# Two-layer encoder on one core: seven block products for eight in twelve of the 44 pairs of W_up blocks

## The chip, the cores and the metric

The kernel runs on one core of a Trainium2 chip. The metric is the device time of the whole program in microseconds, the median of several runs. One further execution is recorded by the hardware profiler; its engines are PE (TensorE, matrix products), DVE (VectorE), ACT (ScalarE), POOL (GpSimd) and SP (SyncE, which issues most DMAs).

## The reference

Two layers, each an attention and Fourier block followed by a feed-forward block. The change touches the second of these alone:

```python
h = rmsnorm(x, norm2[l])                                   # 512 positions x 1024
up = dwconv_centred(h @ w_up[l], conv_w[l], conv_b[l])     # 1024 -> 5632, then 3 taps along positions
gate, val = up[..., :D_FF], up[..., D_FF:]                 # D_FF = 2816
x = x + (jax.nn.silu(gate) * val) @ w_down[l]
```

Everything is float32.

## The kernel before, in words

Activations lie with channels on the 128 partitions and the 512 positions in the free dimension. A float32 matrix is split into hi (rounded to the format in which PE multiplies fast) and lo = value - hi, and `mm3` makes each product from three matmuls: hi by hi, lo by hi, hi by lo (L120, L121, L122). ACT writes a hi, DVE the lo (`split` for activations, `wsplit` for weights: `whi` and `wlo`, five buffers each, half a tile of 1024 columns at a time). Raw weights arrive by DMA in `wraw`, three buffers.

The feed-forward block has 22 gate and 22 value tiles of W_up; gate tile `fi` and value tile `fi + 22` are a pair. For each tile a PSUM bank collects 8 x 3 matmuls of 128x512, so a pair has 48. A chunk, the 12 matmuls that use one `whi`/`wlo`, is half a tile. After a tile DVE multiplies by the positions' 1/rms (`rb2`, into a `tF` tile), ACT starts the convolution with its middle tap (`tF<-tF,pb`), and DVE adds the other two taps (L96, `scalar_tensor_tensor`). Once both tiles of a pair are there, ACT applies silu, the two are multiplied (by DVE in layer 0, by POOL in layer 1), and the result is split into `slab`, `pT` or `m4` for W_down. There are six `tF` buffers. The pairs come in two halves of eleven (`HALVES`); after each half follow the products with W_down, eight output tiles of 11 x 3 matmuls (the down stage). In layer 0's feed-forward block `presplit(1)` also prepares layer 1's projection weights, and layer 1's rope and other tables are loaded (`load_tables`).

The program is written as plain loops. When it is built, a scheduler fixes for each engine one order of instructions, and assigns buffers and waits; the engines then run independently, each in its own order.

Of the kernel before, what the change touches and what calls it, by code (L numbers as in the profile page):

```python
# [16 lines left out]
P = 128  # L17
# [15 lines left out]
RATE, STEP0 = 1, 12  # L33
FFN_BANKS = ("mm", "mm", "mm", "av", "sc", "sc")
HALVES = [(0, 11), (11, 11)]


def encoder_kernel(tc, t):
# [50 lines left out]
    def act(out, in_, func=AF.Copy, **kw):  # L89
        return nc.scalar.activation(out, in_, func, **kw)  # L90

    def tt(out, a, b, op, eng=None):
        return (eng or nc.vector).tensor_tensor(out, a, b, op=op)  # L93

    def stt(out, a, s, b, op0, op1):
        return nc.vector.scalar_tensor_tensor(out=out, in0=a, scalar=s, in1=b, op0=op0, op1=op1)  # L96
# [17 lines left out]
    def mm3(out, a, b, start, stop, after=None, **kw):  # L114

        with tc.issue_after(after) if after is not None else nullcontext():
            if len(a) == 1:
                nc.tensor.matmul(out, a[0], b[0], start=start, stop=stop, **kw)  # L118
                return
            nc.tensor.matmul(out, a[0], b[0], start=start, stop=False, **kw)  # L120
            nc.tensor.matmul(out, a[1], b[0], start=False, stop=False, **kw)  # L121
            nc.tensor.matmul(out, a[0], b[1], start=False, stop=stop, **kw)  # L122
# [20 lines left out]
    def wchunks(src, n, step=512, eng=None):  # L143
        raw = wload(src, n)
        return [wsplit(raw[:, c:min(c + step, n)], eng) for c in range(0, n, step)]

    kept = {}

    def presplit(l):

        late = []

        def keep(key, src):
            n = src.shape[-1]
            two = [temp(n, "tA", F32R) for _ in range(2)]
            split(two[0], two[1], src)
            kept[key] = [dp.tile([P, n], F32, tag=f"{key}{s}", name=nm("kept")) for s in range(2)]
            store()
            late.append(lambda: [nc.sync.dma_start(o, f(z)) for o, z in zip(kept[key], two)])

        def store():
            while late:
                late.pop()()

        def cols(src, n, step):
            def load():
                raw = temp(1024, "m4")
                nc.sync.dma_start(raw[:, :n], src)
                return [raw[:, c:c + step] for c in range(0, n, step)]
            return load  # L170

        def prepare(kind, raw):
            if kind == "u":
                return fold_wu(raw)
            return fold_wf(raw) if kind == "f" else raw

        jobs = []
        for grp in (1, 0):
            for kk in range(KT // 2):
                jobs.append((cols(t["w_qkv"][l, grp, kk], 768, 384), [f"qkv{grp}{2 * kk + i}" for i in range(2)]))  # L180
        for kk in range(KT // 2):
            jobs.append((lambda kk=kk: load_wu(l, kk, temp(1024, "m4")), [f"u{2 * kk + i}" for i in range(2)]))
        for j in range(NF):
            jobs.append((lambda j=j: [load_wf(l, j, temp(1024, "m4"))], [f"f{j}"]))
        for half in range(2):
            for mp in range(KT // 2):
                jobs.append((cols(t["w_o"][l, half, :, mp * 1024:(mp + 1) * 1024], 1024, 512),
                             [f"o{half}{2 * mp + i}" for i in range(2)]))
        got = jobs[0][0]()
        for n, (_, keys) in enumerate(jobs):  # L190
# [145 lines left out]
    def accum(tag="acc"):  # L336
        return cp.tile([P, 512], F32, tag=tag, name=nm(tag), bufs=1)
# [30 lines left out]
    def load_wu(l, kk, raw=None):  # L368

        raw = wtile() if raw is None else raw  # L370
        nc.sync.dma_start(raw.rearrange("p (k c) -> p k c", k=2),
                          t["w_in"][l, 2 * kk * P:2 * (kk + 1) * P, 0:FW].rearrange("(k p) c -> p k c", p=P))
        return [raw[:, k * 512:(k + 1) * 512] for k in range(2)]

    acc = accum()
    xg = [norm_tile(k, g1[:, 0, :], acc) for k in range(KT)]

    for l in range(L):
# [319 lines left out]
        rb2 = row_rstd(col_rstd(acc2, 1.0 / D))  # L698


        acc = accum()
        if l == 0:
            tabs, alts, wt = load_tables(1)
        ahead = presplit(l + 1) if l < L - 1 else iter(lambda: 0, 1)
        for f0, nf in HALVES:
            gu = []
            for fi in range(f0, f0 + nf):
                ys_ = []
                n = fi - f0
                for z in range(2):  # L710
                    m = fi + z * FT
                    w = wchunks(t["w_up"][l, m], 1024)
                    nps[0] += 1
                    o = psum(FFN_BANKS[nps[0] % len(FFN_BANKS)])
                    for k in range(KT):
                        mm3(o, [q[:, (k % 4) * P:(k % 4 + 1) * P] for q in w[k // 4]], [h2[k][:, s, :] for s in range(2)],
                            k == 0, k == KT - 1)
                    u = temp(512, "tF")
                    tt(u, o, rb2, ALU.mult)
                    y = temp(512, "tF")  # L720
                    act(y, u, AF.Identity, scale=cw[:, l, 1, m:m + 1], bias=cb[:, l, m:m + 1])
                    stt(y[:, 1:], u[:, :-1], cw[:, l, 0, m:m + 1], y[:, 1:], ALU.mult, ALU.add)
                    stt(y[:, :-1], u[:, 1:], cw[:, l, 2, m:m + 1], y[:, :-1], ALU.mult, ALU.add)
                    ys_.append(y)
# [36 lines left out]
            xg = nxt
# [88 lines left out]
```

## Time and profile before

| | us |
|---|---|
| median of 3 runs | 1057.18 (1056.22 to 1057.36) |
| profiled execution | 1056.14 |
| its span | 1054.3 |
| PE busy in the span | 1038.2 |
| DVE busy | 726.8 |
| ACT busy | 507.9 |
| up stages of layer 0, by the trace | 182 to 305 and 362 to 485 |
| up stages of layer 1 | 692 to 812 and 870 to 993 |

The time of an execution is its span and 1.84 us around it. In a group's row stand the line, engine and operation, then output and inputs by the program's names, the shape, the count; behind the first bar the busy time and the mean of one in ns, behind the second the engine's idle time before these instructions and what ended it. A timeline row begins with the start and the duration in us. Matmul durations overlap, so one reads the distance of their starts.

### The profile page before, as it was taken

Reading aid. Unit: us, or ns where it says so; the run is one execution under the profiler, and the core shown is the slowest. Engines: PE = TensorE matmul, PEld = TensorE weight load, DVE = VectorE, ACT = ScalarE, POOL = GpSimd, SP = SyncE. Lnnn points to the kernel's source line nnn. Section 1 sums busy time; section 2 is a strip of 40 time slices with the busy share of each in tenths; the row PEclk is TensorE's granted clock in tenths of the full one; section 3 lists DMA queues with packets and bytes.
Section 4 is the critical chain, followed back from the end, with each engine's and each line's share of the span. In section 5 each row is a group of like instructions: output and inputs, shape, how many; then the busy total and the mean of one; then the engine's idle time right before and its main releaser. Section 6 shows DMA issues by size and latency. Waiting matters only on the chain.

```text
span 1054.3 us, 14425 instructions
## 1 busy us (share of the span) xinstructions
PE 1038.2 (98%) x5107; PEld 873.2 (83%) x5107; DVE 726.8 (69%) x1384; ACT 507.9 (48%) x939; POOL 90.8 (9%) x164
## 2 busy tenths in 40 slices
PE   8998999999999999999999999999999999999998
PEld 8986778888888888888899887888888888888887
DVE  8878768697767777777519775478877336878632
ACT  5339755455444445455423785246554224454421
POOL 0004410000000000000000152001101000101100
PEclk9999999999999999999999999999999999999999
DMA  7232152332269833239856313333332333332241
GB/s 273 83 115 87 58 193 81 100 100 96 78 226 353 324 100 101 89 114 322 280 181 221 113 62 99 122 100 94 101 101 74 96 115 100 98 101 82 82 150 48
DMA packets 60475, 140.03 MB, mean 133 GB/s; under 512 B 6642, under 2 KB 22258, under 8 KB 60404
## 3 DMA queue, kind: packets, MB, share of 16 engines
q1 hardware_dynamic: 60404, 139.12, 40.5%
q8 instruction: 40, 0.66, 0.3%
q14 instruction: 31, 0.25, 0.1%
HBM read 116.02 MB, written 23.07 MB: 132 GB/s over the span
## 4 chain that ended last, share of the span: by engine, by line
PE 93%; DVE 2%; DMA 2%; ACT 1%; issue 1%; POOL 0%; SPq 0%; ACTq 0%; DVEq 0%; POOLq 0%
PE ps L122 28%; PE ps L120 28%; PE ps L121 28%; PE ps L118 3%; PE ps L548 2%; PE ps L541 2%; PE ps L529 1%; DMA wraw<-in_w_qkv_dram 1%; PE ps L234 1%; PE ps L227 1%; ACT tA L90 0%; DMA x<-in_xT_dram 0%; DVE tA L533 0%; ACT act L90 0%; PE ps L500 0%
## 5 line engine op out<-in xcount | busy, mean ns | idle before, releaser
L90 ACT ACTIVATE whi<-wraw 128x512 fp32r<-128x512 f32 (+1 forms) x296 | 182.0, 616 | 290.8 <-PE ps L122 278.4
L120 PE MATMUL ps<-act,whi 128*128 128x512 f32 x768 | 298.9, 390 | 0.0
L121 PE MATMUL ps<-act,wlo 128*128 128x512 f32 x768 | 298.3, 389 | 0.0
L122 PE MATMUL ps<-act,whi 128*128 128x512 f32 x768 | 298.2, 389 | 0.0
L93 DVE TENSOR_TENSOR wlo<-wraw,whi 128x512 fp32r<-128x512 f32 (+1 forms) x304 | 219.7, 726 | 103.4 <-ACT whi L90 102.0
L122 PEld LDWEIGHTS ps<-act,whi 128*128 128x128 f32 x768 | 144.2, 188 | 30.1
L120 PEld LDWEIGHTS ps<-act,whi 128*128 128x128 f32 x768 | 144.2, 188 | 29.7
L121 PEld LDWEIGHTS ps<-act,wlo 128*128 128x128 f32 x768 | 144.2, 188 | 29.7
L96 DVE SCALAR_TENSOR_TENSOR tF<-tF,pb,tF 128x511 f32<-128x511 f32 x176 | 133.5, 763 | 11.1 <-ACT tF L90 8.7
L93 DVE TENSOR_TENSOR tF<-ps,rb 128x512 f32<-128x512 f32 x104 | 71.2, 689 | 77.9 <-PE ps L122 64.7
L120 PE MATMUL ps<-slab,whi 128*128 128x512 f32 (+2 forms) x212 | 82.2, 388 | 0.0
L122 PE MATMUL ps<-slab,whi 128*128 128x512 f32 (+2 forms) x212 | 79.9, 380 | 0.4 <-DVE slab L93 0.3
L121 PE MATMUL ps<-slab,wlo 128*128 128x512 f32 (+2 forms) x212 | 80.0, 378 | 0.0
L90 ACT ACTIVATE tF<-tF,pb 128x512 f32<-128x512 f32 x88 | 71.7, 816 | 11.3 <-DVE tF L93 4.6
L93 DVE TENSOR_TENSOR x<-x,ps 128x512 f32<-128x512 f32 (+1 forms) x49 | 32.9, 674 | 36.5 <-PE ps L122 36.3
L93 POOL TENSOR_TENSOR tF<-tF,tF 128x512 f32<-128x512 f32 x22 | 30.2, 1371 | 256.1 <-DVE tF L96 224.1
L120 PE MATMUL ps<-pT,whi 128*128 128x512 f32 (+1 forms) x132 | 50.5, 383 | 0.0
L121 PE MATMUL ps<-pT,wlo 128*128 128x512 f32 (+1 forms) x132 | 50.5, 383 | 0.0
L122 PE MATMUL ps<-pT,whi 128*128 128x512 f32 (+1 forms) x132 | 50.5, 383 | 0.0
L538 POOL TENSOR_SCALAR tA<-tA,den 128x256 f32<-128x256 f32 (+1 forms) x64 | 37.4, 590 | 145.1 <-DVE den L537 144.6
L533 DVE CUSTOM_DVE_ANT_0 tA<-ps,pb,nsink 128x256 f32<-128x256 f32 (+1 forms) x64 | 37.8, 603 | 14.5 <-PE ps L529 9.7
L122 PEld LDWEIGHTS ps<-slab,whi 128*128 128x128 f32 x212 | 39.7, 188 | 8.3 <-DVE slab L93 0.9
(178 smaller groups left out, 1485.0 us busy)
## 6 DMA issues: line engine op xcount, KB each, us to landing
wraw<-in_w_up_dram SPq DMA_DIRECT2D x88, 512.0 KB, 3.5
wraw<-in_w_down_dram SPq DMA_DIRECT2D x32, 512.0 KB, 3.7
kept<-tA SPq DMA_DIRECT2D x56, 256.0 KB, 5.7
whi<-kept SPq DMA_DIRECT2D x28, 256.0 KB, 3.0
wlo<-kept SPq DMA_DIRECT2D x28, 256.0 KB, 3.0
kept<-tA SPq DMA_DIRECT2D x32, 192.0 KB, 4.4
wraw<-in_w_down_dram SPq DMA_DIRECT2D x32, 192.0 KB, 2.4
wraw<-in_w_o_dram SPq DMA_DIRECT2D x8, 512.0 KB, 3.7
```

What stands on the lines that cost most here:

```text
L90: return nc.scalar.activation(out, in_, func, **kw)
L93: return (eng or nc.vector).tensor_tensor(out, a, b, op=op)
L96: return nc.vector.scalar_tensor_tensor(out=out, in0=a, scalar=s, in1=b, op0=op0, op1=op1)
L118: nc.tensor.matmul(out, a[0], b[0], start=start, stop=stop, **kw)
L120: nc.tensor.matmul(out, a[0], b[0], start=start, stop=False, **kw)
L121: nc.tensor.matmul(out, a[1], b[0], start=False, stop=False, **kw)
L122: nc.tensor.matmul(out, a[0], b[1], start=False, stop=stop, **kw)
L227: nc.tensor.matmul(pt[:, 2 * b:2 * b + 2], acc[:, b * P:(b + 1) * P], ones2, start=True, stop=True)
L533: nc.vector.tensor_tensor_reduce(out=pr[:, :n], in0=sc[:, :n], in1=mask[:, m0:m0 + n], scale=qs_scale[p][:, i, e:e + 1], scalar=nsink[:, l ...
L538: nc.gpsimd.tensor_scalar(pr[:, :n], pr[:, :n], den[:, i:i + 1], 1.0, op0=ALU.mult, op1=ALU.mult)
L541: tr = nc.tensor.transpose(pp[:, j * P:(j + 1) * P], pr[:, j * P:(j + 1) * P], ident)
L548: pv = nc.tensor.matmul(py[64 * e:64 * e + 64, i0 * P:(i1 + 1) * P], vp[:, j, 64 * g:64 * g + 64], pT[:, half, e, b0:b0 + 2 * (i1 - i0) + ...
```

## The change

In twelve pairs, `fi` = 6, 9, 13, 16, 19 of layer 0 and 6, 8, 12, 14, 16, 18, 20 of layer 1, the products of gate and value tile are treated as one 2x2 block matrix, a11 and a12 the halves of the gate tile, a21 and a22 those of the value tile, times the 2x2 block matrix of activations (upper and lower half of the channels by left and right 256 positions). The eight block products become seven, on sums of blocks. They are named here by letters, in the program's order:

| | product | sum of W | added into |
|---|---|---|---|
| A | a11 x B11 | | X, copied by ACT to the gate's left half |
| B | s1 x T1 | s1 = a21 + a22 | Y, copied by ACT to the value's right half |
| C | a12 x B21 | | Z, added by DVE to the gate's left half |
| D | s2 x T2 | s2 = s3 - a22 (s3 below) | X, copied by ACT to the gate's right half |
| E | s4 x B22 | s4 = a12 + s2 | Y |
| F | s3 x T3 | s3 = a11 - a21 | X |
| G | a22 x T4 | | X |

Each product is 12 matmuls of 128x256, 84 in all. X and Y lie in the two `tp` banks. D adds into X, so it must come after ACT has copied A out of X; E must come after the copy of Y, F after the copy of D, G after DVE has read F. Of the sums, made by DVE, s1 and s4 are written over parts of the raw tiles, s2 and s3 into a tile under the tag `ropetab` (`sums`), through which layer 1's weights do not pass. The gate's half goes on to the convolution after F, the value's after G.

T1 to T4 are sums of activation blocks, which `seven_h` makes once for a layer, one k of four after each of the first four pairs: two scaled copies by ACT, four adds of 256 columns by DVE, two hi by ACT and two lo by DVE, into tiles that are free at that time (`room`).

Three other things move. The product of silu(gate) and value goes from POOL to DVE in layer 1. `accum` and `load_tables(1)` move from the start of the feed-forward block to the second down stage of layer 0. And in `presplit` the hi by ACT is ordered behind the last convolution written before it (`pace`). Two lines more at the head shift line numbers by two: L122 to L124 are now the three matmuls of `mm3`, L92 ACT's operations, L95 and L98 DVE's.

The core of the diff:

```diff
+SEVEN = ((6, 9, 13, 16, 19), (6, 8, 12, 14, 16, 18, 20))
...
-            split(two[0], two[1], src)
+            with tc.issue_after(pace[0]) if pace[0] is not None else nullcontext():
+                act(two[0], src)
+            tt(two[1], src, f(two[0]), ALU.subtract)
...
+    def seven_h(k, l, h2, room):
+        b = [temp(512, "tF") for _ in range(2)]
+        for i in range(2):
+            act(b[i], x[k + 4 * i], scale=g2[:, l, k + 4 * i:k + 4 * i + 1])
...
+        t13, t24 = sums_of_b(*b)
+        parts(g, t13, ("T1", "T3"), room)
+        parts(g, t24, ("T2", "T4"), room)
+        return g
...
+    def up_seven(l, fi, h2, ts, rb2):
+        a, b = [wload(t["w_up"][l, fi + z * FT], 1024) for z in range(2)]
+        a11, a12, a21, a22 = a[:, :512], a[:, 512:], b[:, :512], b[:, 512:]
+        nps[0] += 1
+        X, Y, Z = [psum(tag)[:, LO] for tag in ("tp", "tp", FFN_BANKS[nps[0] % len(FFN_BANKS)])]
+        ua, ub = temp(512, "tF"), temp(512, "tF")
+
+        def product(o, w, key, start=False):
+            for k in range(4):
+                mm3(o, [z[:, k * P:(k + 1) * P] for z in w], ts[k][key], start and k == 0, k == 3, skip_group_check=True)
+
+        product(X, wsplit(a11), "B11", True)
+        act(ua[:, LO], X)
+        two = sp.tile([P, 1024], F32, tag="ropetab", name=nm("sums"), bufs=1)
+        s1, s2, s3, s4 = a21, two[:, :512], two[:, 512:], a12
+        tt(s3, a11, a21, ALU.subtract)
+        tt(s1, a21, a22, ALU.add)
+        product(Y, wsplit(s1), "T1", True)
+        act(ub[:, HI], Y)
+        product(Z, wsplit(a12), "B21", True)
+        tt(ua[:, LO], ua[:, LO], Z, ALU.add)
+        tt(s2, s3, a22, ALU.subtract)
+        product(X, wsplit(s2), "T2")
+        act(ua[:, HI], X)
+        tt(s4, a12, s2, ALU.add)
+        product(Y, wsplit(s4), "B22")
+        product(X, wsplit(s3), "T3")
+        tt(ub[:, HI], ub[:, HI], X, ALU.add)
+        tt(ua[:, HI], ua[:, HI], Y, ALU.add)
+        tt(ua, ua, rb2, ALU.mult)
+        yield ua
+        product(X, wsplit(a22), "T4")
+        tt(ub[:, LO], X, rb2[:, LO], ALU.mult)
+        tt(ub[:, HI], ub[:, HI], rb2[:, HI], ALU.mult)
+        yield ub
...
-        acc = accum()
-        if l == 0:
-            tabs, alts, wt = load_tables(1)
...
+                for z, u in enumerate((up_seven if fi in SEVEN[l] else up_eight)(l, fi, h2, ts, rb2)):
+                    ys_.append(conv(l, fi + z * FT, u))
...
+                if SEVEN[l] and len(ts) < 4:
+                    ts.append(seven_h(len(ts), l, h2, room))
                 act(ys_[0], ys_[0], AF.Silu)
-                tt(ys_[0], ys_[0], ys_[1], ALU.mult, nc.gpsimd if l else nc.vector)
+                tt(ys_[0], ys_[0], ys_[1], ALU.mult)
...
             nxt = []
+            if l < L - 1 and f0 + nf == FT:
+                acc = accum()
+                tabs, alts, wt = load_tables(1)
```

How the order of instructions changes is shown at layer 1's `fi` = 6 on three engines and at layer 0's on one. Names carry the scheduler's numbers; what stands in brackets is the engine or queue that an instruction waits for.

ACT in layer 1, near `fi` = 6, before: each `whi` is for a chunk that PE multiplies about four chunks later, and waits until PE has freed its buffer (`whi_1692` for the end of the chunk `whi_1673`).

```order
L90 ACTIVATE whi_1690_7636<-wraw_1689_7634 128x512 [waits DMAHW4_49,PE_49]
L90 ACTIVATE tF_1671_7539<-tF_1670_7537,pb_96 128x512 [waits DVE_49]
L90 ACTIVATE whi_1692_7640<-wraw_1689_7634 128x512 [waits PE_49]
L90 ACTIVATE pT_1655_7458<-tF_1663_7498 128x512 [waits Pool_49]
L90 ACTIVATE whi_1698_7677<-wraw_1697_7675 128x512 [waits DMAHW5_49,PE_49]
```

ACT at the same place now: `whi_1801` and `whi_1803` are the two chunks of a tile of the next pair, `ps_1777` is X, `ps_1778` is Y.

```order
L92 ACTIVATE whi_1801_8145<-wraw_1800_8143 128x512 [waits DMAHW4_49,PE_49]
L92 ACTIVATE tF_1757_7900<-tF_1756_7898,pb_96 128x512 [waits DVE_49]
L92 ACTIVATE tF_1766_7946<-tF_1765_7944,pb_96 128x512 [waits DVE_49,Activation_49]
L92 ACTIVATE tF_1749_7859<-tF_1749_7859 128x512 [waits DVE_49]
L92 ACTIVATE tF_1774_7987<-tF_1773_7985,pb_96 128x512 [waits DVE_49,Activation_49]
L92 ACTIVATE whi_1803_8149<-wraw_1800_8143 128x512 [waits PE_49]
L92 ACTIVATE pT_1758_7906<-tF_1749_7859 128x512 [waits DVE_49]
L92 ACTIVATE tF_1780_8002<-ps_1777_7999 128x256
L92 ACTIVATE tF_1766_7946<-tF_1766_7946 128x512 [waits DVE_49,Activation_49]
L92 ACTIVATE tF_1781_8003<-ps_1778_8000 128x256
```

`whi_1801` waits for the end of C, `whi_1803` for the end of the chunk `whi_1801`, and the copy of X (the row with `ps_1777`) stands behind both and behind the split into `pT_1758`, which waits for the silu product.

PE there before goes from chunk to chunk of one tile:

```order
L120 MATMUL ps_1677_7557<-act_1539_6899,whi_1673_7549 128x512
L121 MATMUL ps_1677_7557<-act_1539_6899,wlo_1674_7550 128x512
L122 MATMUL ps_1677_7557<-act_1539_6899,whi_1673_7549 128x512
L120 MATMUL ps_1677_7557<-act_1547_6929,whi_1675_7553 128x512 [waits Activation_49]
L121 MATMUL ps_1677_7557<-act_1547_6929,wlo_1676_7554 128x512 [waits DVE_49]
```

Now PE goes from the end of C (`ps_1779` is Z) to a chunk of the next pair:

```order
L122 MATMUL ps_1779_8001<-act_1635_7380,whi_1787_8041 128x256
L123 MATMUL ps_1779_8001<-act_1635_7380,wlo_1788_8042 128x256
L124 MATMUL ps_1779_8001<-act_1635_7380,whi_1787_8041 128x256
L122 MATMUL ps_1805_8153<-act_1596_7204,whi_1801_8145 128x512 [waits Activation_49]
L123 MATMUL ps_1805_8153<-act_1596_7204,wlo_1802_8146 128x512 [waits DVE_49]
```

and from that chunk over one matmul of the following one to D:

```order
L122 MATMUL ps_1805_8153<-act_1611_7276,whi_1801_8145 128x512
L123 MATMUL ps_1805_8153<-act_1611_7276,wlo_1802_8146 128x512
L124 MATMUL ps_1805_8153<-act_1611_7276,whi_1801_8145 128x512
L122 MATMUL ps_1805_8153<-act_1619_7306,whi_1803_8149 128x512 [waits Activation_49]
L122 MATMUL ps_1777_7999<-room_1664_7498,whi_1789_8059 128x256 [waits Activation_49]
```

The last row is D's first matmul; it waits for the copy of X.

DVE at this place, before: evacuations, taps and lo halves take turns.

```order
L93 TENSOR_TENSOR wlo_1668_7509<-wraw_1664_7502,whi_1667_7508 128x512 [waits Activation_49]
L93 TENSOR_TENSOR tF_1653_7450<-ps_1652_7425,rb_1569_7023 128x512 [waits PE_49]
L93 TENSOR_TENSOR wlo_1674_7550<-wraw_1672_7547,whi_1673_7549 128x512 [waits DMAHW2_49,Activation_49]
L96 SCALAR_TENSOR_TENSOR tF_1654_7452<-tF_1653_7450,pb_96,tF_1654_7452 128x511 [waits Activation_49]
L96 SCALAR_TENSOR_TENSOR tF_1654_7452<-tF_1653_7450,pb_96,tF_1654_7452 128x511 [waits DVE_49]
L93 TENSOR_TENSOR wlo_1676_7554<-wraw_1672_7547,whi_1675_7553 128x512 [waits Activation_49]
```

DVE now, from the lo of the next pair's first chunk to that of its second: two evacuations, six taps and the silu product of earlier pairs stand between (the product is the row with two `tF` tiles and no `pb`).

```order
L95 TENSOR_TENSOR wlo_1802_8146<-wraw_1800_8143,whi_1801_8145 128x512 [waits DMAHW4_49,Activation_49]
L95 TENSOR_TENSOR tF_1765_7944<-ps_1764_7919,rb_1641_7400 128x512 [waits DVE_49]
L98 SCALAR_TENSOR_TENSOR tF_1757_7900<-tF_1756_7898,pb_96,tF_1757_7900 128x511 [waits Activation_49]
L98 SCALAR_TENSOR_TENSOR tF_1749_7859<-tF_1748_7857,pb_96,tF_1749_7859 128x511 [waits DVE_49]
L98 SCALAR_TENSOR_TENSOR tF_1757_7900<-tF_1756_7898,pb_96,tF_1757_7900 128x511 [waits DVE_49]
L98 SCALAR_TENSOR_TENSOR tF_1766_7946<-tF_1765_7944,pb_96,tF_1766_7946 128x511 [waits Activation_49]
L95 TENSOR_TENSOR tF_1773_7985<-ps_1772_7960,rb_1641_7400 128x512 [waits DVE_49]
L95 TENSOR_TENSOR tF_1749_7859<-tF_1749_7859,tF_1757_7900 128x512 [waits DVE_49,Activation_49]
L98 SCALAR_TENSOR_TENSOR tF_1766_7946<-tF_1765_7944,pb_96,tF_1766_7946 128x511 [waits DVE_49]
L98 SCALAR_TENSOR_TENSOR tF_1774_7987<-tF_1773_7985,pb_96,tF_1774_7987 128x511 [waits Activation_49]
L95 TENSOR_TENSOR wlo_1804_8150<-wraw_1800_8143,whi_1803_8149 128x512 [waits Activation_49]
```

The product stands four taps and three other instructions behind the start of `wlo_1802`.

ACT in layer 0, `fi` = 6, now (`whi_597`, not shown, is the next pair's first chunk and `whi_599` its second, `ps_573` is X):

```order
L92 ACTIVATE tF_548_2419<-tF_547_2417,pb_96 128x512 [waits DVE_49,Activation_49]
L92 ACTIVATE tF_557_2465<-tF_556_2463,pb_96 128x512 [waits DVE_49,Activation_49]
L92 ACTIVATE tF_536_2370<-tF_536_2370 128x512 [waits DVE_49]
L92 ACTIVATE tF_565_2506<-tF_564_2504,pb_96 128x512 [waits DVE_49,Activation_49]
L92 ACTIVATE tA_566_2510<-m4_494_2203 128x384 [waits DMAHW1_49]
L92 ACTIVATE whi_599_2678<-wraw_596_2672 128x512 [waits PE_49]
L92 ACTIVATE tF_557_2465<-tF_557_2465 128x512 [waits DVE_49,Activation_49]
L92 ACTIVATE tF_576_2531<-ps_573_2528 128x256
```

The copy of X, the last row, stands behind three convolutions, of which the third waits for a tap of DVE, and behind two silus.

More of the change, by code (lines that the diff above doesn't have):

```diff
@@ L147, in encoder_kernel @@
     kept = {}
+    pace = [None]
     def presplit(l):
@@ L373, in load_wu, with sums_of_b, parts @@
         return [raw[:, k * 512:(k + 1) * 512] for k in range(2)]
+    LO, HI = slice(0, 256), slice(256, 512)
+    def sums_of_b(b1, b2):
+        t13, t24 = temp(512, "tF"), temp(512, "tF")
+        tt(t13[:, LO], b1[:, HI], b1[:, LO], ALU.subtract)
+        tt(t13[:, HI], b2[:, HI], b1[:, HI], ALU.subtract)
+        tt(t24[:, LO], t13[:, LO], b2[:, HI], ALU.subtract)
+        tt(t24[:, HI], t24[:, LO], b2[:, LO], ALU.add)
+        return t13, t24
+    def parts(g, src, keys, room):
+        two = [next(room), next(room)]
+        split(*two, src)
+        for key, cols in zip(keys, (LO, HI)):
+            g[key] = [z[:, cols] for z in two]
@@ new lines, in h_rooms @@
+    def h_rooms(l):
+        for tag in ("th0", "th1", "tl0", "tl1", "wt0", "wt1", "v", "accA", "accF", "acc"):
+            yield cp.tile([P, 512], F32R, tag=tag, name=nm("room"), bufs=1)
+        yield cp.tile([P, 512], F32R, tag="rb", name=nm("room"), bufs=2)
+        for _ in range(2):
+            yield tp.tile([P, 516], F32R, tag="tail", name=nm("room"), bufs=2)[:, :512]
+        for _ in range(2):
+            yield temp(512, "sq", F32R)
+        yield cp.tile([P, 512], F32R, tag="room", name=nm("room"), bufs=1)
@@ new lines, in seven_h, with up_eight @@
+    def seven_h(k, l, h2, room):
+        b = [temp(512, "tF") for _ in range(2)]
+        for i in range(2):
+            act(b[i], x[k + 4 * i], scale=g2[:, l, k + 4 * i:k + 4 * i + 1])
+        g = dict(B11=[z[:, LO] for z in halves(h2[k])], B21=[z[:, LO] for z in halves(h2[k + 4])],
+                 B22=[z[:, HI] for z in halves(h2[k + 4])])
+        t13, t24 = sums_of_b(*b)
+        parts(g, t13, ("T1", "T3"), room)
+        parts(g, t24, ("T2", "T4"), room)
+        return g
+    def up_eight(l, fi, h2, ts, rb2):
+        for z in range(2):
+            w = wchunks(t["w_up"][l, fi + z * FT], 1024)
+            nps[0] += 1
+            o = psum(FFN_BANKS[nps[0] % len(FFN_BANKS)])
+            for k in range(KT):
+                mm3(o, [q[:, (k % 4) * P:(k % 4 + 1) * P] for q in w[k // 4]], [h2[k][:, s, :] for s in range(2)],
+                    k == 0, k == KT - 1)
+            u = temp(512, "tF")
+            tt(u, o, rb2, ALU.mult)
+            yield u
@@ new lines, in up_seven @@
+    def up_seven(l, fi, h2, ts, rb2):
+        a, b = [wload(t["w_up"][l, fi + z * FT], 1024) for z in range(2)]
+        a11, a12, a21, a22 = a[:, :512], a[:, 512:], b[:, :512], b[:, 512:]
+        nps[0] += 1
+        X, Y, Z = [psum(tag)[:, LO] for tag in ("tp", "tp", FFN_BANKS[nps[0] % len(FFN_BANKS)])]
[27 more added lines that the diff above has]
+        yield ub
@@ L375, in encoder_kernel, with conv @@
+    def conv(l, m, u):
+        y = temp(512, "tF")
+        pace[0] = act(y, u, AF.Identity, scale=cw[:, l, 1, m:m + 1], bias=cb[:, l, m:m + 1]).ins
+        stt(y[:, 1:], u[:, :-1], cw[:, l, 0, m:m + 1], y[:, 1:], ALU.mult, ALU.add)
+        stt(y[:, :-1], u[:, 1:], cw[:, l, 2, m:m + 1], y[:, :-1], ALU.mult, ALU.add)
+        return y
     acc = accum()
@@ L698, in encoder_kernel @@
         rb2 = row_rstd(col_rstd(acc2, 1.0 / D))
-        acc = accum()
-        if l == 0:
-            tabs, alts, wt = load_tables(1)
         ahead = presplit(l + 1) if l < L - 1 else iter(lambda: 0, 1)
+        room, ts = h_rooms(l), []
         for f0, nf in HALVES:
@@ L709, in encoder_kernel @@
                 n = fi - f0
[L710 to L724, printed above, removed]
+                for z, u in enumerate((up_seven if fi in SEVEN[l] else up_eight)(l, fi, h2, ts, rb2)):
+                    ys_.append(conv(l, fi + z * FT, u))
                     if (2 * n + z) % 3 == 2:
                         next(ahead)
+                if SEVEN[l] and len(ts) < 4:
+                    ts.append(seven_h(len(ts), l, h2, room))
                 act(ys_[0], ys_[0], AF.Silu)
-                tt(ys_[0], ys_[0], ys_[1], ALU.mult, nc.gpsimd if l else nc.vector)
+                tt(ys_[0], ys_[0], ys_[1], ALU.mult)
                 if n < 4:
```

## Prediction

> **What bounds the kernel now.** I read the head of the page first, then the slices, the chain that ended last, the waits of PE, and then windows over the two feed-forward stages, where the change lies.
>
> ```profile
> span 1054.3 us, 14425 instructions
> PE 1038.2 (98%) x5107; PEld 873.2 (83%) x5107; DVE 726.8 (69%) x1384; ACT 507.9 (48%) x939; POOL 90.8 (9%) x164
> PEclk9999999999999999999999999999999999999999
> PE 93%; DVE 2%; DMA 2%; ACT 1%; issue 1%; POOL 0%; SPq 0%; ACTq 0%; DVEq 0%; POOLq 0%
> PE ps L274 <- ACT sq L90: 2.7, 1, 2.7
> PE ps L234 <- POOL nr L211: 1.5, 1, 1.5
> ```
>
> PE is busy 98% of the span and is 93% of the chain; the granted clock is full in all 40 slices. Its longest wait anywhere is 2.7 us (total, times, longest stand behind the colon). The windows (busy time of PE, PEld, DVE, ACT, POOL, then granted clock, DMA share, GB/s) are the up stages of layer 0 (first, third) and of layer 1 (fourth, fifth); the second is layer 0's first down stage:
>
> ```profile
> 184.00:305.00 121.00, 121.00 (x544) 100.42 (x543) 89.53 (x137) 61.04 (x94) 1.01 (x1) 1.00 0.32 100
> 305.00:362.00 57.00, 57.00 (x253) 47.22 (x252) 41.77 (x90) 25.42 (x45) 0.00 (x0) 1.00 1.01 356
> 362.00:485.00 123.00, 123.00 (x545) 101.83 (x544) 90.96 (x135) 61.12 (x93) 0.00 (x0) 1.00 0.38 119
> 690.00:812.00 122.00, 122.00 (x547) 101.26 (x546) 97.04 (x136) 63.23 (x96) 14.89 (x11) 1.00 0.30 94
> 870.00:993.00 123.00, 123.00 (x544) 101.83 (x544) 93.90 (x122) 59.49 (x88) 12.88 (x10) 1.00 0.30 93
> ```
>
> PE has no gap at all in 489 us of up work, nor in the down stage, whose DMA share is 1.01. So only two things can move the time here: less PE work, and new gaps on PE. DVE, at 89.5 of 121 us, is the engine with least room.
>
> **What the change removes: PE time.** These rows, first and last of 15 and of 63 starts one after another, give the pitch of both shapes:
>
> ```profile
> 299.75 0.39 PE L121 MATMUL ps<-pT,wlo 128*128 128x512 f32 x1
> ...
> 302.93 0.39 PE L120 MATMUL ps<-slab,whi 128*128 128x512 f32 x1
> 1042.98 0.28 PE L120 MATMUL ps<-slab,whi 128*128 128x256 f32 x1
> ...
> 1050.42 0.28 PE L122 MATMUL ps<-m,whi 128*128 128x256 f32 x1
> ```
>
> 3.18 us over 14 steps is 0.227 us for 512 columns, and 7.44 over 62 is 0.120 for 256. A pair by eight products is 48 x 0.227 = 10.90 us, one by seven 84 x 0.120 = 10.08. That is 0.82 less a pair, and **-9.8 us** for twelve. Both shapes load fresh weights for each matmul, so this carries over.
>
> **What it adds: work on DVE and ACT.**
>
> ```profile
> L93 DVE TENSOR_TENSOR wlo<-wraw,whi 128x512 fp32r<-128x512 f32 x116 | 97.4, 841 | 50.4 <-ACT whi L90 49.8
> L93 POOL TENSOR_TENSOR tF<-tF,tF 128x512 f32<-128x512 f32 x22 | 30.2, 1371 | 256.1 <-DVE tF L96 224.1 <-ACT whi L90 19.2 <-ACT tF L90 12.8
> L93 DVE TENSOR_TENSOR tF<-tF,tF 128x512 f32<-128x512 f32 x22 | 15.1, 685 | 0.0
> L93 DVE TENSOR_TENSOR whi<-wraw 128x256 f32<-128x256 f32 x8 | 3.0, 416 | 0.0
> L90 ACT ACTIVATE tF<-tF,pb 128x512 f32<-128x512 f32 x44 | 35.9, 816 | 5.5 <-DVE tF L93 1.8 <-DVE tF L96 0.6
> L90 ACT ACTIVATE pT<-ps 128x256 f32<-128x256 f32 x32 | 12.1, 378 | 7.7 <-PE ps L541 7.3
> 235.12 0.69 DVE L93 TENSOR_TENSOR tF<-ps,rb 128x512 f32<-128x512 f32 x1 [0.76 <-PE ps L122]
> 235.73 0.68 DVE L93 TENSOR_TENSOR pT<-tF,pT 128x512 fp32r<-128x512 f32 x1
> 208.68 0.75 DVE L96 SCALAR_TENSOR_TENSOR tF<-tF,pb,tF 128x511 f32<-128x511 f32 x1
> 209.34 0.69 DVE L93 TENSOR_TENSOR tF<-ps,rb 128x512 f32<-128x512 f32 x1
> ```
>
> Queued DVE work goes by starts, not by durations: a 512-wide tensor_tensor every 0.605 us (235.12 to 235.73), a conv tap every 0.66 (208.68 to 209.34). For 256 columns (0.42 alone) I estimate 0.335, half of 0.605 and the same fixed part; for 384, 0.47. An eight has 4 lo halves, 2 evacuations, the product, the lo of its result and 4 taps: 8 x 0.605 + 4 x 0.66 = 7.5 us of DVE. A seven has 7 lo, 4 sums of W, 3 more of 512 and 5 of 256, and 4 taps: 14 x 0.605 + 5 x 0.335 + 2.64 = 12.8. One of each, as they alternate in layer 1's second half, is 20.3 us of DVE beside 20.98 of PE. seven_h adds 4 x 0.335 + 2 x 0.605 = 2.55 to each of the first four pairs of a layer. In total DVE just fits; it no longer has lead.
>
> The POOL product of layer 1 goes to DVE: 22 x 0.605 = 13.3 us more, against the lo halves there, 841 ns in layer 1; at the 685 of the third row they would give back up to 116 x 0.156 = 18 us. Between -5 and +13 us of DVE; I take zero. The tables' work (now in layer 0's second down stage) and the ordered presplit: zero, since PE did not wait even in the 1.01 DMA window; at most the 1.5 us of the nr wait.
>
> **What it makes PE wait for.** Four hops, from layer 0:
>
> ```profile
> 226.97 0.63 ACT L90 ACTIVATE whi<-wraw 128x512 fp32r<-128x512 f32 x1 [1.11 <-PE ps L122]
> 227.50 0.61 ACT L90 ACTIVATE slab<-tF 128x512 fp32r<-128x512 f32 x1
> 225.52 0.69 DVE L93 TENSOR_TENSOR tF<-tF,tF 128x512 f32<-128x512 f32 x1
> 229.26 0.39 PE L122 MATMUL ps<-act,whi 128*128 128x512 f32 x1
> 229.69 0.63 ACT L90 ACTIVATE whi<-wraw 128x512 fp32r<-128x512 f32 x1 [1.57 <-PE ps L122]
> 230.22 0.61 ACT L90 ACTIVATE tF<-tF 128x512 f32<-128x512 f32 x1
> 230.35 0.69 DVE L93 TENSOR_TENSOR wlo<-wraw,whi 128x512 fp32r<-128x512 f32 x1
> 198.99 0.48 PE L121 MATMUL ps<-act,wlo 128*128 128x512 f32 x1
> 199.91 0.69 DVE L93 TENSOR_TENSOR tF<-ps,rb 128x512 f32<-128x512 f32 x1 [2.43 <-ACT rb L90]
> ```
>
> The last matmul of a chunk to the hi split that waits for its slot is 0.43 us (229.26 to 229.69), hi to lo 0.66, the lo itself 0.69, ACT's pitch 0.53. The first three rows show what a queue does: the slab's hi had its input at 226.21 (225.52 + 0.69), yet started at 227.50, behind a whi that waited for PE. In the kernel before, that costs PE nothing, because a chunk is split some four chunks ahead. In the order of the changed kernel this lead is gone at five places, and D and its likes wait for ACT's copy out of X, which stands in that same queue.
>
> Layer 1, fi = 6. The next chunk's slot is freed by C, the product just ahead on PE: 0.43 + 0.66 + 0.69 less the one matmul that needs no lo and C's own step, 0.35, is 1.4 us; I take 1.7, since DVE has a lo and more in front. Then, counting from the start of that chunk's lo, its twelfth matmul starts at 0.7 + 10 x 0.227 = 2.97, and D could at 3.4. But the copy stands behind a slab hi that waits for the silu product, and DVE works off 3 x 0.605 + 4 x 0.66 before that: it starts at 4.5, ends at 5.2, slab hi to 5.7, copy to 6.1, D at 6.2: 2.8. Together **4.5**.
>
> Layer 0, fi = 6. From the end of the rb transposes (198.99) PE has 182 x 0.227 + 36 x 0.120 = 45.6 us before it needs the lo of the following eight's first chunk. DVE, which starts 0.92 later, has 83 instructions before that lo in its order: 47 x 0.605 + 17 x 0.66 + 16 x 0.335 + 3 x 0.47 = 46.4, then 0.69: 48.0. PE waits 2.3 (at least the 1.4 above). Then D's copy stands behind a conv that waits for the fourth of the taps on DVE (started 4.4 after the lo, done at 5.2), then conv 0.72 (0.82 less overlap), a 384 copy 0.45, a whi 0.53, a silu 0.53, and the copy 0.45: D at 8.0 for 3.4: 4.6. Together **6.9**.
>
> Layer 0, fi = 9: one matmul of the next eight, then D, whose copy is fifth in ACT's queue behind a whi that waits for C: 0.43 + 0.53 + 0.72 + 0.45 + 0.53 + 0.38 = 3.05, less 0.35: **2.7**. Layer 1, fi = 8: a chunk of the next eight, put ahead of D, whose slot B frees: 1.4 and another lo and silu in front, **2.3**. The other sevens have only a short wait of the copy behind one hi, 0.3 to 0.45 each: **0.85** in layer 0 and **1.5** in layer 1.
>
> The sum is 6.9 + 2.7 + 0.85 + 4.5 + 2.3 + 1.5 = 18.8 us of gaps, less 9.8: **+9.0 us**. The profiled execution was 1056.14 (1054.3 and 1.84 around it), 1.04 below the median 1057.18; so the forecast is 1065.1 on its base and **1066.2** on the median's. With the least values (1.4 at both starts, 2.3 falling to 1.4) the gaps are 16.7, hence 1064.1; with 24 (every lo with one more DVE instruction of 0.6 in front, twelve times, and 2 more at the start) 1071.4.
>
> A rule bears on the largest gap. In the rows above PE's longest wait is 2.7 us and the clock stays full. The Trainium skill ("TensorE: Matmul & The Clock Gate", "Why this matters for your kernels") says that PE idle for more than about 3 us falls back to half rate; by it the 4.6 us gap would be followed by about 3.4 us at half rate, an estimated 1.7 us more, 1067.9. No row here shows it. I leave it out of the sum and give it 1 in 5.
>
> **Rivals.** *All hidden, faster.* If ACT and DVE regain their lead by fi = 6, the copies are ready when C ends, and -9.8 stands: 1047.4. For it: PE's 489 us without a gap beside a DVE at three quarters. Against it: DVE's 46.4 us beside PE's 45.6, with no idle time in it, and five chunks that wait for the product just ahead, whatever DVE does. It decides where the gaps sum to less than 7.7 us.
>
> *Only the lead is lost.* If the copies' waits (4.6, 2.7, 2.8 and the 2.35 of the late ones) come to nothing because the taps and silus ahead of them are done early, 6.35 us remain: 1053.7. For it: before, taps run soon after their evacuation. Against it: the copies stand behind them in ACT's own order.
>
> By the Trainium skill (the same page, Part 1, "Architectural detail") ACT and DVE queues are strict first-in, first-out; the 227.50 row agrees, its wait of 1.29 us being for nothing else. Were it not so, the case just named would be the likely one.
>
> *DVE becomes the bound.* If queued DVE work goes by durations, not starts, one eight and one seven cost 22 x 0.685 + 5 x 0.416 + 8 x 0.75 = 23.2 us, 2.2 over PE, five times in layer 1's second half: 11 more, 1077. Against it are the starts 0.605 apart. Half of it is possible where operands are late.
>
> That the change does not do what it says is excluded: the order of PE holds twelve pairs of 84 narrow matmuls.
>
> **Chances.** Gaps of 14 to 24 us, 1061 to 1072: 0.64, and 1066.2 is its centre. The clock's 1.7 us stays within that band. DVE bound, above it: 0.11. Only the lead lost: 0.09, half of it above 1055.1, so that it counts as the same. All hidden: 0.10. Something between, 1055 to 1061: 0.06. This kernel can tell 0.2%, 2.1 us, from nothing; so faster 0.15, same 0.08, slower 0.77. The range 1056 to 1076 leaves out the fast cases and a little at the top.
>
> **What would show it.** Right: in the changed kernel's waits PE waits for ACT at D and for DVE at the eight's lo, some 7 us at fi = 6 of layer 0 and 4 to 5 us at that of layer 1; two matmul pitches of 0.227 and 0.120; DVE over 0.9 busy in layer 1's second half, PE without gaps of more than 0.5 us there. Wrong: those gaps missing or under 8 us together; a 256-wide pitch that is not 0.120 beside the weight splits; a clock below full after the long gap; gaps at the sums of W.

## The result and the profile after

The changed kernel takes 1069.68 us (median of 4 runs, 1068.46 to 1070.29) against 1056.97 for the kernel before in the same series: ratio 1.0119, 95% interval [1.0107, 1.0131], 12.7 us slower. The forecast on the median's base was 1066.2, in a range of 1056 to 1076. The profiled execution's span grew by 13.6 us.

The head of the page and PE's waits, after:

```profile
span 1067.9 us, 15610 instructions
PE 1037.1 (97%) x5539; PEld 889.6 (83%) x5539; DVE 787.4 (74%) x1586; ACT 544.1 (51%) x1043; POOL 60.3 (6%) x142
PEclk9999999998999999999999999999999999999999
PE 88%; DVE 6%; ACT 3%; issue 1%; DMA 1%; POOL 0%; SPq 0%; ACTq 0%; DVEq 0%; POOLq 0%
PE ps L122 <- ACT whi L92: 7.8, 6, 2.5
PE ps L123 <- DVE wlo L95: 3.8, 3, 1.5
PE ps L122 <- ACT tF L92: 2.6, 5, 1.4
```

The three waits are new: for the hi of a chunk, for its lo, and (`tF`) for the copy out of X. They sum to 14.2 us. One slice of the granted clock, the tenth, is below full. PE's busy time has fallen by only 1.1 us, though 9.8 us of matmul starts are gone. Two things fill the other 8.7 us. About half are matmuls that ran at half rate. The rest stands at the edges of the gaps, where the page still counts a matmul as busy although the next should already have started: set against the starts, as below, the gaps sum to 18.4 us and not to 14.2.

Timeline of PE in layer 1 at `fi` = 6: the last matmul of C, the next eight's first chunk (whi_1801) from its first matmul to its last, the first matmul of whi_1803, then D.

```profile
769.36 0.28 PE L124 MATMUL ps<-act,whi 128*128 128x256 f32 x1
770.36 0.50 PE L122 MATMUL ps<-act,whi 128*128 128x512 f32 x1 [0.72 <-ACT whi L92]
771.97 0.50 PE L123 MATMUL ps<-act,wlo 128*128 128x512 f32 x1 [1.10 <-DVE wlo L95]
...
774.38 0.39 PE L124 MATMUL ps<-act,whi 128*128 128x512 f32 x1
777.24 0.51 PE L122 MATMUL ps<-act,whi 128*128 128x512 f32 x1 [2.47 <-ACT whi L92]
778.02 0.51 PE L122 MATMUL ps<-room,whi 128*128 128x256 f32 x1 [0.28 <-ACT tF L92]
778.33 0.42 PE L123 MATMUL ps<-room,wlo 128*128 128x256 f32 x1
778.55 0.41 PE L124 MATMUL ps<-room,whi 128*128 128x256 f32 x1
778.76 0.41 PE L122 MATMUL ps<-room,whi 128*128 128x256 f32 x1
...
780.68 0.63 PE L123 MATMUL ps<-act,wlo 128*128 128x512 f32 x1
781.11 0.60 PE L124 MATMUL ps<-act,whi 128*128 128x512 f32 x1
```

Read the starts: 0.12 would follow each 256-wide matmul and 0.227 each 512-wide one. After 769.36 the next two start 0.88 and 1.38 too late, after 774.38 the next two 2.63 and 0.55 too late. Then D runs with 0.21 between starts, and the matmul at 780.68 takes 0.43 to the next: half rate, until about 781.5.

What ACT and DVE did in the second gap:

```profile
772.43 2.73 DVE L98 SCALAR_TENSOR_TENSOR tF<-tF,pb,tF 128x511 f32<-128x511 f32 x4
775.07 0.68 DVE L95 TENSOR_TENSOR tF<-ps,rb 128x512 f32<-128x512 f32 x1
775.67 0.68 DVE L95 TENSOR_TENSOR tF<-tF,tF 128x512 f32<-128x512 f32 x1
775.85 0.81 ACT L92 ACTIVATE tF<-tF,pb 128x512 f32<-128x512 f32 x1 [1.35 <-DVE tF L95]
776.57 0.61 ACT L92 ACTIVATE whi<-wraw 128x512 fp32r<-128x512 f32 x1
777.09 0.62 ACT L92 ACTIVATE pT<-tF 128x512 fp32r<-128x512 f32 x1
777.61 0.36 ACT L92 ACTIVATE tF<-ps 128x256 f32<-128x256 f32 x1
```

The hi of whi_1803 could have gone at 774.8, when PE freed its buffer, but stood behind a conv that waited for the evacuation at 775.07. The copy out of X (777.61) stood behind the hi and the split into `pT`. A's last matmul had started at 766.50, so A had been in X for more than 10 us.

Windows of the changed kernel (columns as in the prediction): `fi` = 6 of layer 0, of layer 1, and the alternating half of layer 1, whose up stage runs from 887.6 to 1004.2.

```profile
240.00:260.00 20.00, 15.06 (x73) 12.15 (x72) 18.81 (x32) 11.99 (x22) 0.00 (x0) 0.83 0.37 118
765.00:785.00 20.00, 15.42 (x86) 13.16 (x85) 18.44 (x32) 11.18 (x20) 0.00 (x0) 0.91 0.27 79
888.00:1004.00 116.00, 115.77 (x707) 103.71 (x706) 105.05 (x179) 65.89 (x114) 0.00 (x0) 1.00 0.33 98
```

In the two bad places PE is busy three quarters of the time, the clock at 0.83 and 0.91, DVE over 0.9. In the third, with its five alternating sevens, PE is all but gapless beside a DVE that is 0.91 busy.

### The profile page after: what moved, and what is told of

It is laid out like the page before. It is cut to its first block, busy times and chain, and to the rows that moved or that the text cites. A ratio compares the mean times of both kernels' runs of the same rounds, so it can differ in the third digit from the quotient of the medians.

```text
span 1067.9 us, 15610 instructions
## 1 busy us (share of the span) xinstructions
PE 1037.1 (97%) x5539; PEld 889.6 (83%) x5539; DVE 787.4 (74%) x1586; ACT 544.1 (51%) x1043; POOL 60.3 (6%) x142
## 4 chain that ended last, share of the span: by engine, by line
PE 88%; DVE 6%; ACT 3%; issue 1%; DMA 1%; POOL 0%; SPq 0%; ACTq 0%; DVEq 0%; POOLq 0%
PE ps L122 26%; PE ps L124 26%; PE ps L123 26%; PE ps L120 3%; PE ps L654 2%; PE ps L647 2%; PE ps L635 1%; DVE tF L98 1%; DVE wlo L95 1%; DVE tF L95 1%; ACT tF L92 1%; ACT tA L92 1%; PE ps L240 1%; DVE tA L639 0%; ACT act L92 0%
## 5 line engine op out<-in xcount | busy, mean ns | idle before, releaser
L92 ACT ACTIVATE whi<-wraw 128x512 fp32r<-128x512 f32 (+1 forms) x308 | 188.2, 615 | 271.7 <-PE ps L124 242.1
L95 DVE TENSOR_TENSOR wlo<-wraw,whi 128x512 fp32r<-128x512 f32 (+1 forms) x316 | 209.7, 668 | 109.6 <-ACT whi L92 108.5
L122 PE MATMUL ps<-act,whi 128*128 128x512 f32 (+1 forms) x720 | 265.1, 371 | 7.8 <-ACT whi L92 7.8
L123 PE MATMUL ps<-act,wlo 128*128 128x512 f32 (+1 forms) x720 | 266.1, 371 | 3.8 <-DVE wlo L95 3.8
L124 PE MATMUL ps<-act,whi 128*128 128x512 f32 (+1 forms) x720 | 265.8, 370 | 0.0
L122 PEld LDWEIGHTS ps<-act,whi 128*128 128x128 f32 x720 | 136.0, 189 | 32.2 <-ACT whi L92 9.8
L123 PEld LDWEIGHTS ps<-act,wlo 128*128 128x128 f32 x720 | 136.6, 190 | 27.4 <-DVE wlo L95 4.8
L124 PEld LDWEIGHTS ps<-act,whi 128*128 128x128 f32 x720 | 136.4, 189 | 21.9
L98 DVE SCALAR_TENSOR_TENSOR tF<-tF,pb,tF 128x511 f32<-128x511 f32 x176 | 128.2, 746 | 1.9 <-ACT tF L92 1.5
L122 PE MATMUL ps<-slab,whi 128*128 128x512 f32 (+2 forms) x212 | 81.8, 386 | 0.0
L92 ACT ACTIVATE tF<-tF,pb 128x512 f32<-128x512 f32 x88 | 70.5, 807 | 20.4 <-DVE tF L95 15.8
L124 PE MATMUL ps<-slab,whi 128*128 128x512 f32 (+2 forms) x212 | 79.3, 379 | 0.3 <-DVE slab L95 0.3
L95 DVE TENSOR_TENSOR tF<-ps,rb 128x512 f32<-128x512 f32 (+1 forms) x92 | 58.5, 649 | 27.0 <-PE ps L124 13.9
L95 DVE TENSOR_TENSOR x<-x,ps 128x512 f32<-128x512 f32 (+1 forms) x49 | 32.7, 672 | 41.1 <-PE ps L124 40.8
L122 PE MATMUL ps<-room,whi 128*128 128x256 f32 x168 | 48.4, 288 | 2.9 <-ACT tF L92 2.6
L122 PE MATMUL ps<-pT,whi 128*128 128x512 f32 (+1 forms) x132 | 50.5, 383 | 0.0
L124 PE MATMUL ps<-pT,whi 128*128 128x512 f32 (+1 forms) x132 | 50.5, 383 | 0.0
L124 PE MATMUL ps<-room,whi 128*128 128x256 f32 x168 | 48.0, 286 | 0.0
L123 PE MATMUL ps<-room,wlo 128*128 128x256 f32 x168 | 47.8, 284 | 0.0
```

## The experiments

Each is set beside the kernel before, run on the same chip. Medians in us:

| kernel | median | ratio to before, 95% interval |
|---|---|---|
| changed kernel | 1069.68 | 1.0119 [1.0107, 1.0131] |
| e1_none: no seven | 1056.27 | 0.9989 [0.9979, 0.9998] |
| e2_sums: no seven, sums made | 1055.95 | 0.9987 [0.9977, 0.9996] |
| e3_late: 8 late sevens | 1051.98 | 0.9951 [0.9936, 0.9966] |
| e4_fill: idle matmuls in the gaps | 1067.97 | 1.0102 [1.0086, 1.0117] |
| e5_early: 4 early sevens alone | 1074.05 | 1.0160 [1.0144, 1.0175] |
| e6_moved: 12 sevens elsewhere | 1058.90 | 1.0017 [1.0007, 1.0026] |
| e7_nocopy: D in a bank of its own | 1054.46 | 0.9973 [0.9963, 0.9983] |
| e8_fill_short | 1069.17 | 1.0111 [1.0096, 1.0126] |
| e9_ten: 10 late sevens | 1049.65 | 0.9927 [0.9914, 0.9941] |

**The parts of the change without sevens.**

```diff
-SEVEN = ((6, 9, 13, 16, 19), (6, 8, 12, 14, 16, 18, 20))
+SEVEN = ((), ())
```

> No seven in either layer and no seven_h; the other parts of the change stay (silu product from POOL to DVE in layer 1, tables later, presplit ordered). Theory (all of the loss lies in the sevens): 1057 us, within 1 of before, DVE's lo halves in layer 1 back to about 690 ns. Rival (the move from POOL or of the tables costs): 1059 to 1062.

It took 1056.27, 1.2 less than its before (1057.45). The silu product on DVE and the moved tables cost nothing and may gain a little. As expected, the lo halves of layer 1's weights took 0.69 us each (0.85 and 0.93 in its two up stages before), which pays for the product on DVE: DVE's busy time is 718.1 us against 726.8.

**The sums of activations alone.**

```diff
+SEVEN = ((), ())
...
-                if SEVEN[l] and len(ts) < 4:
+                if len(ts) < 4:
```

> As e1_none, but seven_h makes its sums of activations after the first four pairs of each layer; nobody reads them. Theory: DVE has no more lead, but an eight only asks for its lo halves four chunks ahead, so PE does not wait: 1057, at most 1059. Rival (DVE's backlog alone stops PE): two gaps of 2 us or more a layer, 1061 or more.

1055.95, no gap. This is DVE at its fullest in layer 0's first up stage:

```profile
182.00:306.00 124.00, 124.00 (x556) 102.94 (x555) 103.54 (x174) 73.17 (x122) 1.01 (x1) 1.00 0.39 129
```

DVE is busy 103.5 of 124 us and PE all 124. DVE's backlog by itself stops nothing, as long as only eights follow.

**Late sevens, early sevens.**

```diff
+SEVEN = ((13, 16, 19), (12, 14, 16, 18, 20))   # e3_late
+SEVEN = ((6, 9), (6, 8))                       # e5_early
```

> Sevens only at fi = 13, 16, 19 of layer 0 and 12, 14, 16, 18, 20 of layer 1. Theory (the loss is the gaps and the slow clock at the four early ones): 8 x -0.82 = -6.6, and gaps of 2 x 0.48 and 3 x 0.34, so 1052.5 us; granted clock at full. Rival (DVE has no room beside alternating sevens): 1057 or more.

> Only the four early sevens, fi = 6 and 9 of layer 0, 6 and 8 of layer 1. Theory (each early seven loses a set of gaps whatever the others do): 1056.3 of the kernel without sevens, less 4 x 0.82, plus gaps of 16.5, plus 0 to 4.4 of half-rate matmuls: 1069.5 to 1074. Rival (the early gaps come from the number of sevens that follow): under 1062.

Both theories held: 1051.98 for 1052.5, and 1074.05 at the upper end of 1069.5 to 1074. Eight late sevens gain, four early ones cost 17 us, more than all twelve do in the changed kernel. In e3_late the only gaps left at the sevens are 2 of 0.48 us in layer 0 and 3 of 0.34 in layer 1.

**D without the wait for the copy.**

```diff
+        nps[0] += 1
+        X = psum(FFN_BANKS[nps[0] % len(FFN_BANKS)])[:, LO]
-        product(X, wsplit(s2), "T2")
+        product(X, wsplit(s2), "T2", True)
```

> The changed kernel with D, F and G in a PSUM bank of their own, so that D need not wait for ACT's copy of A out of X (A is then missing from the gate's right half and from the value). Theory (D's wait for that copy is the root: because D cannot go, a chunk of the next pair is put ahead and its weights lose their lead): the gaps at the four early sevens shrink from 16.5 to 4 at most, the clock stays full, 1049 to 1053. Rival (DVE is behind at fi = 6 for its own reasons and the eight's lo is late in any case): gaps of 2 us and more stay, 1058 or more.

1054.46: nearer to the theory, though 1.5 above its upper end. PE's waits now:

```profile
PE ps L122 <- ACT whi L92: 1.8, 3, 0.8
PE ps L123 <- DVE wlo L95: 1.5, 3, 0.7
PE ps L122 <- ACT tF L92: 0.8, 2, 0.6
```

In its order D follows C at once, no chunk of the next pair is put between (but for one matmul), and weights are split at least 1.3 us of PE work ahead in all places but one, at `fi` = 6 of layer 0. In the feed-forward blocks no matmul runs at half rate. So 15.2 of the 1069.68 hang on that wait and on the order that follows from it. What is left at the four early sevens, about 6 us in gaps of 0.5 to 0.9 us by the starts, where the theory allowed 4 at most, is the lateness of DVE and ACT that the rival spoke of.

**Useless work in the gaps.**

```diff
+FILL = {(0, 6): 40, (0, 9): 20, (1, 6): 40, (1, 8): 20}    # e8_fill_short: {(0, 6): 22, (1, 6): 17}
         product(Z, wsplit(a12), "B21", True)
+        for _ in range(FILL.get((l, fi), 0)):
+            nc.tensor.matmul(Zb[:, HI], h2[0][:, 0, :P], h2[0][:, 0, LO], start=True, stop=True, skip_group_check=True)
```

> The changed kernel with useless matmuls of 128x256 put behind C of the four early sevens (40 each at fi = 6 of both layers, 20 each at fi = 9 of layer 0 and fi = 8 of layer 1; 14.4 us of PE work), into the unused half of Z's bank. Theory (PE stands idle there for ACT and DVE, and idling lowers the clock): the gaps of 16.5 us shrink to 2 to 5, the 4.4 us of half-rate matmuls vanish, so 1063 to 1066 us although PE does 14.4 us more, clock 1.00. Rival (the half rate has another cause, not idling): the slow matmuls stay, 1068 to 1071. Rival (the gaps are not waits that other work can cover): 1080 or more.

> The changed kernel with 22 useless matmuls of 128x256 behind C at fi = 6 of layer 0 and 17 at that of layer 1 (2.6 and 2.0 us), as much as the first of the two gaps there; the second gap is left. The work done in the gap costs nothing, so any difference is the clock. Theory A (idling within some 10 us adds up, so without the first gap the clock holds): 4.4 us less than the changed kernel, 1065.3. Theory B (the second gap of 3.2 us lowers the clock alone): 1.1 us less or nothing, 1068.5 to 1069.7, slow matmuls behind the second gap.

e4_fill took 1067.97: with 14.4 us of work more it is no slower than the changed kernel, the clock is full in all slices, and of the waits remain

```profile
PE ps L123 <- ACT whi L93: 1.6, 2, 0.8
PE ps L124 <- DVE wlo L96: 1.1, 3, 0.4
PE ps L123 <- ACT tF L93: 0.9, 3, 0.3
```

So the gaps are idleness that other work can take, and without them no matmul ran at half rate. The time is 2 us over the range that I gave, in part because half-rate matmuls inside a gap cost nothing: in layer 0 the chunk between the two gaps ran slowly, but the hi that PE waited for next came from ACT and DVE at its own time. e8_fill_short bears this out. Its fills took away the first gap's slow stretch, the second gap still slowed D in both layers (starts 0.21 apart at 256 columns and 0.43 at 512, from 254.3 to 257.7 and from 776.5 to 779.9), and the time was 1069.17, as theory B had it.

**Twelve sevens at other places.**

```diff
+SEVEN = ((10, 13, 16, 19), (10, 11, 12, 13, 14, 16, 18, 20))
```

> Twelve sevens as in the changed kernel, at fi = 10, 13, 16, 19 of layer 0 and 10, 11, 12, 13, 14, 16, 18, 20 of layer 1, where no chunk's hi split waits for the product just ahead of it. Theory (the place of the sevens, not their number, makes the gaps): 1056.3 - 9.8 + 2 to 3 of short gaps, 1048.5 to 1050. Rival (twelve sevens are too much for DVE, four in a row above all): gaps of 2 us and more at 11 to 13 of layer 1, 1053 or more.

The theory failed: 1058.90, and the rival's gaps are there, where the sevens at `fi` = 12, 13 and 14 of layer 1 begin.

```profile
PE ps L122 <- DVE tF L95: 5.8, 4, 2.1
PE ps L122 <- ACT tF L92: 1.5, 3, 0.8
PE ps L122 <- ACT whi L92: 1.1, 1, 1.1
```

The first wait is another than before. This is the first of its gaps, on PE (G's last matmul, then the first of the next seven's B) and on DVE:

```profile
878.93 0.28 PE L124 MATMUL ps<-room,whi 128*128 128x256 f32 x1
880.80 0.39 PE L122 MATMUL ps<-room,whi 128*128 128x256 f32 x1 [1.59 <-DVE tF L95]
880.33 0.42 DVE L95 TENSOR_TENSOR tF<-ps,rb 128x256 f32<-128x256 f32 x1
```

B's Y takes the `tp` bank that was X for the seven before, so B waits until DVE has read G out of it. That read was late because DVE, with about 12.8 us of work (the prediction's count) for each 10.08 us of PE, falls behind as soon as sevens follow one another. Weights split ahead are not enough; a seven also needs an eight beside it.

**Ten sevens.**

```diff
+SEVEN = ((10, 13, 16, 19), (10, 12, 14, 16, 18, 20))
```

> Sevens at fi = 10, 13, 16, 19 of layer 0 and 10, 12, 14, 16, 18, 20 of layer 1: the late eight of e3_late and the last pair before each first down stage. Theory (a seven costs nothing where DVE has run off its backlog and the next work of PE is already split): two more savings of 0.82, 1050.3 to 1051. Rival (fi = 10 stands too near the first four pairs, or the down stage waits for its result): gaps of 2 us and more there, 1052.5 or more.

1049.65, 0.7% faster than before and 20 us faster than the changed kernel: the fastest of all. It is e6_moved without the sevens at `fi` = 11 and 13 of layer 1, and 9 us faster than that. Its alternating half, with PE full and DVE at 0.91:

```profile
870.00:990.00 120.00, 119.77 (x725) 107.03 (x724) 109.31 (x184) 68.54 (x119) 0.00 (x0) 1.00 0.31 97
```

The two sevens at `fi` = 10 caused no gap. The down stage behind them asks less of DVE: 31 of 48 us in layer 0 (312 to 360), 21 of 50 in layer 1 (815 to 865).

**The clock once more.**

> The changed kernel once more, for its clock. Theory (whether a gap of 2 to 3 us lowers the clock depends on when it falls): the same gaps at the same places to 0.1 us, but half-rate matmuls behind another choice of them, 0 to 6 stretches of about 1.6 us each. Rival (the clock is set by the instruction stream): the same three stretches, at fi = 6 of both layers.

The rival came true in these two executions: the same three stretches ran slowly (the chunk and D at `fi` = 6 of layer 0, D at `fi` = 6 of layer 1). But in e5_early the gap at `fi` = 9 of layer 0, of the same size, was followed by one, in the changed kernel not. Windows of the two, e5_early first, each 284 to 294 us:

```profile
284.00:294.00 10.00, 7.82 (x42) 6.58 (x42) 9.34 (x18) 4.82 (x10) 0.00 (x0) 0.83 0.60 197
```

```profile
284.00:294.00 10.00, 7.82 (x55) 6.97 (x54) 9.60 (x17) 6.13 (x12) 0.00 (x0) 1.00 0.49 160
```

The same 7.82 us busy, with 42 matmuls in the one and 55 in the other, at a clock of 0.83 and 1.00. What differs is where the gap falls. In each trace the stretches at half rate last 3.41 us and begin whole multiples of 3.41 us apart: in the changed kernel at 249.06, 255.89 and 778.13, that is 2 and 153 steps. Cut into such steps, the place looks like this (e5_early, then the changed kernel):

```profile
285.83:289.24 3.41, 1.77 (x11) 1.46 (x12) 3.41 (x7) 2.88 (x7) 0.00 (x0) 1.00 0.85 276
289.24:292.66 3.42, 3.42 (x11) 2.75 (x10) 2.76 (x8) 0.90 (x2) 0.00 (x0) 0.50 0.76 291
```

```profile
283.19:286.61 3.42, 2.65 (x22) 2.43 (x20) 3.42 (x7) 1.78 (x4) 0.00 (x0) 1.00 0.23 75
286.61:290.02 3.41, 2.00 (x14) 1.71 (x14) 3.41 (x7) 2.44 (x6) 0.00 (x0) 1.00 0.63 205
290.02:293.43 3.41, 3.41 (x23) 3.08 (x23) 3.05 (x6) 1.61 (x4) 0.00 (x0) 1.00 0.42 153
```

In e5_early both waits fall into one step, which leaves PE busy for 1.77 us of it, and the next step runs at half rate. In the changed kernel the border between two steps, at 286.61, divides the waits, and neither step is emptied enough. So the theory is not refuted: e10_again could not tell, because its steps lay within 0.1 us of the changed kernel's (a border 0.88 us behind D's first matmul at `fi` = 6 of layer 0, against 0.97).

## Why the prediction came out, point by point

**The saving.** 0.120 and 0.227 held: the alternating half and D's first matmuls at `fi` = 6 of layer 0 show them where the clock is full. e3_late and e9_ten give the size in time: from 1056.27 without sevens, eight gain 4.3 us and ten 6.6, where 0.82 each less the five short gaps (2 x 0.48 + 3 x 0.34 = 2.0) makes 4.6 and 6.2.

**The gaps.** Set against the starts on PE (each start beyond its pitch):

| place | predicted | measured |
|---|---|---|
| layer 0, 6: the eight's first chunk | 2.3 | 2.85 |
| layer 0, 6: D and the chunk ahead of it | 4.6 | 3.2, and 1.1 of slow matmuls that it hides |
| layer 0, 9 | 2.7 | 2.6 |
| layer 0, others | 0.85 | 0.96 |
| layer 1, 6: first chunk | 1.7 | 2.26 |
| layer 1, 6: D | 2.8 | 3.2 |
| layer 1, 8 | 2.3 | 2.4 |
| layer 1, others | 1.5 | 1.0 |

That is 18.8 predicted and 18.4 measured, or 19.5 with the hidden part. The sum agrees better than its terms, which are off by up to 1.4 us both ways and cancel; so much of the closeness is luck. Places and releasers are those of the sum, with two corrections. At both `fi` = 6 I let D wait for the copy alone, but most of the second gap (2.22 and 2.47 us) came one matmul earlier, at the hi of the next chunk, which stood in the same queue ahead of the copy. And in layer 1 it was not the split into `pT`, waiting for the silu product, that held the queue: the product was done at 776.35, before that split's turn at 777.09. The conv ahead of the hi held it, which could not start before the evacuation of 775.07 was done. Both first gaps came out 0.55 longer than taken, at the lo: at 246.51 and 770.62 DVE worked off two lo one behind the other, the seven's own last one first.

Two sums are off. The 2.3 at the first chunk of layer 0 is 2.4 by its own terms. And the upper case adds 12 x 0.6 and 2 to 18.8, which is 28.0 us of gaps and 1075.4, not 24 and 1071.4; the range to 1076 covers that as well.

**The clock.** The term that was mis-sized. I left half rate out of the sum at 1 in 5, and priced it at 1.7 us; a clock below full after the long gap was one of my signs of being wrong, and it came. Behind both D it cost 1.6 each, 3.2 us, nearly the 3.7 by which the change exceeds its forecast of +9.0; e4_fill and e7_nocopy, with no wait above 0.8 us there, have none of it. The Trainium skill ("TensorE: Matmul & The Clock Gate", "Why this matters for your kernels") names about 3 us of idling; by that, no gap here would have counted, the longest single wait at a seven being 2.47. The measurement decides: waits of 1.9 to 2.5 us, and pairs of waits that together last 2.2 to 2.5, were followed by half rate where a step of 3.41 us was left half empty, and others of the same size were not.

**The rivals.** *All hidden* is refuted for the early places and true for the late ones. *Only the lead is lost* did not happen: D waits for the copy at three of the four early sevens and at five of the eight late ones. Nor are lead and copy two things, since the copy's wait is what loses the lead: e7_nocopy takes that wait away, and the first gaps shrink with it (2.85, 2.26 and 2.40 to 1.9, 0.83 and 0.80). *DVE becomes the bound* did not happen in the alternating half (PE 115.77 of 116); it did at four sevens in a row. My sign that DVE would be over 0.9 in the alternating half held: 105.05 of 116 is 0.91. POOL's product moved at no cost, as taken.

## What to carry to other kernels

When a step replaces PE work by more work on ACT and DVE, the saving is kept only where its new waits are answered ahead of time. Follow the first instruction that the new step makes PE wait for, and count what stands ahead of it in its engine's queue, not how long it takes itself: here the wait for a 0.36 us copy cost 15 us. The same step at places where the helpers have run off their backlog, with a plain step between, gave 0.7%.

## What the runs showed of the hardware

Half rate came in stretches of 3.41 us, which begin on a grid of 3.41 us that is fixed within one execution (249.06, 255.89 and 778.13 in the changed kernel), with starts 0.21 apart for 256 columns and 0.43 for 512. In the feed-forward blocks of all traces there are 13 such stretches, and before each PE was busy for at most 1.77 us of the step of the grid ahead of it. Of the other steps there, one had PE busy for less than that (1.69 us, e6_moved from 905.75), all the rest for 1.82 us and more. So it is the share of a step that PE is busy, and not the longest wait, that goes with the clock: steps of 1.62 us and less were all followed by half rate, from 1.69 to 1.77 it went either way, and where the border lies exactly these traces do not show. What a gap of 2 us costs thus depends on where it falls. One more stretch, 27 us into the changed kernel, is in e1_none too, so the sevens are not its cause.

Useless matmuls in such a gap keep the rate: e4_fill does 14.4 us more of PE work and ends no later.
